# A hybrid encoder layer on one core: the decays between tokens come from running sums read back from DRAM as rows

## The chip, the core and the metric

The kernel runs on one core of a Trainium2 chip. The core has five engines that run their own instruction streams in order and meet through semaphores: TensorE (PE, matrix products into PSUM), VectorE (DVE), ScalarE (ACT), GpSimd (POOL) and SyncE (SP, which here only issues DMAs). The metric is the device time of one execution in microseconds, the median of several runs.

## The reference, cut to what matters

One layer over 256 tokens of width 2048: RMSNorm, a large input projection, three branches (a bidirectional Mamba-2 scan called SSD, a dilated window attention, a Conformer convolution), gates, an output projection and an MLP with squared ReLU. The change is in the SSD branch, which runs once forward and once backward over two chunks of 128 tokens, with 32 heads of 64 channels in 4 groups. For one direction:

```python
def ssd_chunked(xh, dt, a, bm, cm):
    ...
    adt = (dt * a).reshape(bsz, nc, q, ng, nr).transpose(0, 3, 4, 1, 2)
    a_cs = jnp.cumsum(adt, axis=-1)
    seg = a_cs[..., :, None] - a_cs[..., None, :]
    lower = jnp.tril(jnp.ones((q, q), dtype=bool))
    lmat = jnp.exp(jnp.where(lower, seg, -jnp.inf))
    ...
    cb = jnp.einsum("bclgn,bcsgn->bgcls", cc, bc)
    y_diag = jnp.einsum("bgrcls,bcsgrp->bclgrp", cb[:, :, None] * lmat, xdt)
```

`adt` is negative. For tokens l >= s of a chunk the decay is exp(sum of adt over s < i <= l), a 128 x 128 matrix for each head, chunk and direction. The backward direction needs the same with the tokens reversed, so that for one head and chunk the forward decays fill one triangle and the backward decays the other.

## The kernel before

**The stream of weights.** Nearly all of the time goes to matrix products of f32 weights. The weights come in 696 *units* of up to 512 KB (`load`, L1180, a DMA on SP's queue into one of 5 buffers `raw`). `split` (L1196) makes each into a high part on ACT (`hi`, L1211, type f32r, 4 buffers) and a low part, the difference, on DVE (`lo`, L255 through `split_lo`). `mm` (L1227) multiplies three times: high weight by high and low activation, low weight by high activation (L1264 to L1276). The main loop (L1303) does for each unit k: load unit k + 5, split unit k + 3 (`LEAD`), multiply unit k.

**The jobs.** Everything else is written as generators, the *jobs*, which a planner (`Sched`, L79) advances between the units. A job yields what it needs next: "v", "a", "g" or "p" with a number of nanoseconds (credit on DVE, ACT, POOL or PE, which each unit grants anew), "w" (wait so many units), "b" (PSUM banks, of 4), "m" (slabs of SBUF, of 33), "j" (a condition). Jobs of a lower number go first. The order in which instructions are written is fixed when the program is built; each engine then runs its own in that order.

**job_dt** (L368) makes, once, the step sizes `dt` and `adt = dt * a` for all tokens on the partitions and 64 columns (32 heads, two directions). `adt` is then split into `adh` (f32r, ACT, L428) and `adl` (DVE, L431). Four matmuls with triangular masks (L436) give sums over tokens, whose exponentials `sp` (L440) scale what goes from chunk to chunk.

**job_cb** (L773) makes for one group the product of C and B, masked by the two triangles. **job_ssd** (L796) runs for each of the 4 groups and 2 chunks, eight times. It multiplies x by `sp` (`xsx`, L811) on DVE and by the skip factor on POOL (L813), multiplies by the other chunk's part (L819) and adds both into y (L822, L825). Then it goes through its 8 heads in two half-batches of 4 (`hb`, L826). Each half-batch:

- ACT scales the masks LE and GE by `adh`, one column for each head and direction: 8 instructions (L832) into `rh`; DVE does the same with `adl`, 4 heads at a time: 2 instructions (L835) into `rl`.
- PE multiplies four times with the strict masks `gtr` and `ltr` (f32r copies of GT and LT) into one bank (L842). Entry (s, 4 heads x l) of the bank is the sum of adt between s and l: forward above the diagonal, backward below it.
- ACT scales `cb` by the forward `dt` (L846) and takes the exponential of the bank (L849); DVE adds the backward part of `cb` (L854) and multiplies the two (L857).
- PE multiplies by x (L864), DVE adds the result to y (L869).

The jobs of one group run at priority 3; the long convolution on DVE (`job_conv31`, L551) and its LayerNorm run at priority 4 beside them.

Of the kernel before, what the change touches and what calls it, by code (L numbers as in the profile page):

```python
# [20 lines left out]
P = 128  # L21
# [169 lines left out]
def kernel(ctx: ExitStack, tc: tile.TileContext, xT, xn, par, cm, cd, cq, w1, wq, ws, out):  # L191
# [7 lines left out]
    lp = ctx.enter_context(tc.tile_pool(name="lp", bufs=4))  # L199
    pm = ctx.enter_context(tc.tile_pool(name="pm", bufs=2, space=PSUM))  # L200
    pd = ctx.enter_context(tc.tile_pool(name="pd", bufs=BANKS, space=PSUM))
    ctx.enter_context(tc.manual_schedule())
    cnt = [0]

# [31 lines left out]
    V.memset(ones, 1.0)  # L236
    onesd = cp.tile([P, P], F32, name="onesd")
    V.memset(onesd, 1.0 / D)
    ltr = cp.tile([P, P], F32R, name="ltr")
    gtr = cp.tile([P, P], F32R, name="gtr")  # L240
    qgs = cp.tile([P, 1], F32, name="qgs")
    warm = cp.tile([P, 1], F32, name="warm")

# [124 lines left out]
    def job_dt(main):  # L368
# [6 lines left out]
        raw = tmp[:, 5:7, :].rearrange("p a b -> p (a b)")  # L375
        dt = cp.tile([P, 2, 64], F32, name="dt")
        adt = cp.tile([P, 2, 64], F32, name="adt")
        adh = cp.tile([P, 2, 64], F32R, name="adh")
        adl = cp.tile([P, 2, 64], F32, name="adl")
        ea = cp.tile([P, 64], F32, name="ea")  # L380
        sp = cp.tile([P, 4, HEADS], F32, name="sp")
        st.update(dt=dt, adh=adh, adl=adl, sp=sp)
        yield "j", lambda: "r1" in st
        yield "v", 400
        for t in range(2):
# [38 lines left out]
            V.scalar_tensor_tensor(adt[:, t, :], dt[:, t, :], -1.0, ea, op0=ALU.mult, op1=ALU.mult)  # L424
        S.give(2)
        yield "w", 1
        yield "a", 200
        A.activation(adh, adt, AF.Copy)  # L428
        yield "w", 1
        yield "v", 200  # L430
        V.tensor_tensor(adl, adt, adh.bitcast(F32), op=ALU.subtract)  # L431
        yield "b", 1
        ps = bank((4, P))
        yield "p", 900
        for i, m in enumerate((GT, LE, LT, GE)):
            PE.matmul(ps[:, i, :], m, adt.rearrange("p a b -> p (a b)"), start=True, stop=True)  # L436
        yield "w", 1
        yield "a", 1500
        for i, o in enumerate((0, 64, 96, 32)):
            A.activation(sp[:, i, :], ps[:, i, o:o + HEADS], AF.Exp)  # L440
        S.banks += 1
        yield "w", 1
        yield "v", 300
        V.tensor_tensor(sp[:, 0, :], sp[:, 0, :], dt[:, 0, 0:32], op=ALU.mult)
# [351 lines left out]
    def job_ssd(g, c):  # L796

        yield "j", lambda: cbs[g] is not None
        dt, adh, adl, sp = st["dt"], st["adh"], st["adl"], st["sp"]
        yield "m", 4  # L800
        rh = slab([2, 4, P], F32R, name="rh")
        rl = slab([2, 4, P], F32R, name="rl")
        em = slab([2, 4, P], name="em")
        xsx = slab([2, 512], name="xsx")
        cb, x, yy = cbs[g], xs[g], y[g][:, c, :]
# [18 lines left out]
        yield "v", 620  # L824
        V.tensor_tensor(yy, yy, xsx[:, 1, :], op=ALU.add)  # L825
        for hb in range(2):  # L826
            for d in range(2):
                for i in range(4):
                    col = 32 * d + 8 * g + 4 * hb + i
                    msk = LE if d == 0 else GE  # L830
                    yield "a", 290
                    A.activation(rh[:, d, i, :], msk, AF.Copy, scale=adh[:, c, col:col + 1].bitcast(F32))  # L832
                col = 32 * d + 8 * g + 4 * hb
                yield "v", 620
                V.tensor_tensor(rl[:, d], msk[:, None, :].to_broadcast([P, 4, P]),  # L835
                                adl[:, c, col:col + 4][:, :, None].to_broadcast([P, 4, P]), op=ALU.mult)
            yield "w", 1
            yield "b", 1
            ba = bank((4, P))
            yield "p", 900  # L840
            for n, (lt, src) in enumerate(((gtr, rh[:, 0]), (gtr, rl[:, 0]), (ltr, rh[:, 1]), (ltr, rl[:, 1]))):
                PE.matmul(ba, lt, src, start=(n == 0), stop=(n == 3))  # L842
            for i in range(4):
                yield "a", 290
                col = 8 * g + 4 * hb + i
                A.activation(em[:, 1, i, :], cb[:, c, :], AF.Copy, scale=dt[:, c, col:col + 1])  # L846
            yield "w", 1
            yield "a", 500
            A.activation(em[:, 0], ba, AF.Exp)  # L849
            S.banks += 1  # L850
            for i in range(4):
                yield "v", 270
                col = 32 + 8 * g + 4 * hb + i
                V.scalar_tensor_tensor(em[:, 1, i, :], cb[:, 2 + c, :], dt[:, c, col:col + 1], em[:, 1, i, :],  # L854
                                       op0=ALU.mult, op1=ALU.add)
            yield "v", 620
            V.tensor_tensor(em[:, 0], em[:, 0], em[:, 1], op=ALU.mult)  # L857
            yield "w", 1
            yield "b", 1
            bd = bank((4, P))  # L860
            yield "p", 880
            for i in range(4):
                pr = 256 * hb + 128 * (i // 2)
                PE.matmul(bd[:, i, :], em[:, 0, i, :], x[:, c, pr:pr + P], start=True, stop=True)  # L864
            yield "w", 1
            yield "v", 400
            bv = bd.rearrange("p (q r) e -> p q (r e)", q=2).rearrange("p q (s e) -> p q s e", s=4)[:, :, 0::3, :]
            yv = yy[:, 256 * hb:256 * hb + 256].rearrange("p (q s e) -> p q s e", q=2, s=2)
            V.tensor_tensor(yv, yv, bv, op=ALU.add)  # L869
            S.banks += 1  # L870
# [432 lines left out]
    for k in range(NU):  # L1303
# [9 lines left out]
            nc.scalar.dma_start(dist, cd)  # L1313
        elif k == 8:
            V.tensor_scalar(qgs, par_("qg"), P ** -0.5, None, op0=ALU.mult)
            A.activation(ltr, LT, AF.Copy)
            A.activation(gtr, GT, AF.Copy)
        split(k + LEAD)
        mm(k)
        bi, u = units[k]  # L1320
# [80 lines left out]
```

## Time and profile before

| | |
|---|---|
| median of 3 runs | 1981.73 us |
| lowest and highest | 1981.35 and 1984.19 us |
| the profiled execution | 1983.86 us |
| its span, first to last instruction | 1982.1 us |
| TensorE clock granted, mean | 0.999 |
| moved by DMA | 364.51 MB, 184 GB/s |

The profile is of one execution. Its page gives, for each engine, the busy time and its share of the span; then the span in 40 equal slices, each with a digit for the tenths of the slice in which the engine was busy; then the chain of work that ended last, followed back from the last instruction. A row of a group reads: line, engine, operation, output <- inputs, shapes, count | busy us, mean ns of one | idle time of the engine just before. Instructions of one engine overlap a little, so that busy time can be less than count times mean. A row of the waits reads: who waited <- for whom: us in total, times, longest us. A row of a timeline reads: start us, duration us, engine, line, operation. Lines are those of the kernel printed above.

### The profile page before, as it was taken

Reading aid. Unit: us, or ns where it says so; the run is one execution under the profiler, and the core shown is the slowest. Engines: PE = TensorE matmul, PEld = TensorE weight load, DVE = VectorE, ACT = ScalarE, POOL = GpSimd, SP = SyncE. Lnnn points to the kernel's source line nnn. Section 1 sums busy time; section 2 is a strip of 40 time slices with the busy share of each in tenths; the row PEclk is TensorE's granted clock in tenths of the full one; section 3 lists DMA queues with packets and bytes.
Section 4 is the critical chain, followed back from the end, with each engine's and each line's share of the span. In section 5 each row is a group of like instructions: output and inputs, shape, how many; then the busy total and the mean of one; then the engine's idle time right before and its main releaser. Section 6 shows DMA issues by size and latency. Waiting matters only on the chain.

```text
span 1982.1 us, 29949 instructions
## 1 busy us (share of the span) xinstructions
PE 1966.0 (99%) x11798; PEld 1766.0 (89%) x11798; DVE 1309.0 (66%) x1847; ACT 1036.0 (52%) x1446; POOL 47.5 (2%) x42
## 2 busy tenths in 40 slices
PE   8999999999999999999999999999999999999999
PEld 7999999999998888888888888999988998998887
DVE  5778887887887889896654555555555554455443
ACT  6654576777757655545654444544443443344332
POOL 0000010000000000003000000000000000000000
PEclk9999999999999999999999999999999999999999
DMA  8555554554554555555555556555555555555554
GB/s 284 184 175 183 165 185 145 167 172 144 184 170 161 176 181 178 183 191 187 190 191 183 189 189 207 194 186 192 188 190 189 189 191 191 188 186 191 190 181 149
DMA packets 105342, 364.51 MB, mean 184 GB/s; under 512 B 11760, under 2 KB 12272, under 8 KB 105200
## 3 DMA queue, kind: packets, MB, share of 16 engines
q1 hardware_dynamic: 103904, 360.23, 55.4%
q10 hardware_dynamic: 1296, 2.36, 0.3%
q8 instruction: 92, 1.51, 0.3%
q14 instruction: 50, 0.41, 0.1%
HBM read 360.45 MB, written 2.10 MB: 183 GB/s over the span
## 4 chain that ended last, share of the span: by engine, by line
PE 95%; DVE 0%; issue 0%
PE main L1273 19%; PE main L1274 19%; PE main L1276 19%; PE main L1266 11%; PE main L1264 11%; PE main L1268 11%; PE b L842 1%; PE b L864 1%; PE b L968 1%; PE b L1273 0%; PE b L1274 0%; PE b L1276 0%; PE b L819 0%; PE b L501 0%; PE b L757 0%; PE b L742 0%
## 5 line engine op out<-in xcount | busy, mean ns | idle before, releaser
L255 DVE TENSOR_TENSOR lo<-raw,hi 128x1024 fp32r<-128x1024 f32 (+2 forms) x697 | 831.5, 1194 | 643.5 <-ACT hi L1211 638.7
L1211 ACT ACTIVATE hi<-raw 128x1024 fp32r<-128x1024 f32 (+2 forms) x695 | 716.2, 1032 | 868.7 <-PE main L1274 487.8
L1273 PE MATMUL main<-hi,hh 128*128 128x512 f32 (+1 forms) x800 | 306.1, 383 | 0.0
L1274 PE MATMUL main<-hi,hl 128*128 128x512 f32 (+1 forms) x800 | 299.0, 374 | 0.0
L1266 PE MATMUL main<-x2l,hi 128*128 128x256 f32 x1024 | 246.4, 281 | 0.0
L1264 PE MATMUL main<-x2h,hi 128*128 128x256 f32 x1024 | 246.3, 279 | 0.0
L1266 PE MATMUL main<-hl,hi 128*128 128x256 f32 x896 | 216.3, 281 | 3.2 <-DVE hl L255 3.2
L1264 PE MATMUL main<-hh,hi 128*128 128x256 f32 x896 | 217.7, 282 | 0.0
L565 DVE SCALAR_TENSOR_TENSOR co<-cin,cpar,co 128x256 f32<-128x256 f32 x480 | 211.1, 491 | 0.0
L1276 PE MATMUL main<-lo,hh 128*128 128x512 f32 (+1 forms) x800 | 200.5, 372 | 0.0
L1264 PEld LDWEIGHTS main<-x2h,hi 128*128 128x128 f32 x1024 | 192.7, 188 | 0.2
L1266 PEld LDWEIGHTS main<-x2l,hi 128*128 128x128 f32 x1024 | 192.6, 188 | 0.2
L1273 PE MATMUL main<-hi,ah 128*128 128x512 f32 x480 | 188.9, 394 | 0.0
L1274 PE MATMUL main<-hi,al 128*128 128x512 f32 x480 | 188.6, 393 | 0.0
L1273 PEld LDWEIGHTS main<-hi,hh 128*128 128x128 f32 x800 | 152.5, 191 | 23.4 <-ACT hi L1211 1.2
L1274 PEld LDWEIGHTS main<-hi,hl 128*128 128x128 f32 x800 | 152.2, 190 | 22.9 <-issue 1.9
L1266 PEld LDWEIGHTS main<-hl,hi 128*128 128x128 f32 x896 | 168.8, 188 | 4.2 <-DVE hl L255 3.6
L1264 PEld LDWEIGHTS main<-hh,hi 128*128 128x128 f32 x896 | 169.2, 189 | 0.6
L1276 PEld LDWEIGHTS main<-lo,hh 128*128 128x128 f32 x800 | 148.0, 190 | 22.1
L1268 PE MATMUL main<-x2h,lo 128*128 128x256 f32 x1024 | 138.3, 277 | 0.0
L1276 PE MATMUL main<-lo,ah 128*128 128x512 f32 x480 | 130.1, 393 | 0.0
L1268 PEld LDWEIGHTS main<-x2h,lo 128*128 128x128 f32 x1024 | 127.6, 188 | 0.0
(244 smaller groups left out, 2304.5 us busy)
## 6 DMA issues: line engine op xcount, KB each, us to landing
raw<-ws_dram SPq DMA_DIRECT2D x600, 512.0 KB, 3.3
raw<-wq_dram SPq DMA_DIRECT2D x88, 384.0 KB, 3.1
raw<-w_dram SPq DMA_DIRECT2D x7, 448.0 KB, 7.0
xr<-xn_dram SPq DMA_DIRECT2D x4, 512.0 KB, 9.2
x<-xn_dram SPq DMA_DIRECT2D x4, 512.0 KB, 4.3
xt<-xT_dram SPq DMA_DIRECT2D x7, 256.0 KB, 7.0
out_dram<-x SPq DMA_DIRECT2D x4, 256.0 KB, 3.7
out_dram<-x ACTq DMA_DIRECT2D x4, 256.0 KB, 5.6
```

What stands on the lines that cost most here:

```text
L255: V.tensor_tensor(lo, raw, hi.bitcast(F32), op=ALU.subtract)
L565: V.scalar_tensor_tensor(dst[:, e, :], x[:, e, k:k + T], par_("dw", (2 * i + e) * 31 + k), dst[:, e, :], op0=ALU.mult, op1=ALU.add)
L842: PE.matmul(ba, lt, src, start=(n == 0), stop=(n == 3))
L864: PE.matmul(bd[:, i, :], em[:, 0, i, :], x[:, c, pr:pr + P], start=True, stop=True)
L968: PE.transpose(b[:, e, t * P:t * P + P], src[:, t, k * P:k * P + P], ID)
L1211: A.activation(h, r, AF.Copy)
L1264: PE.matmul(o, wh[:, e, cs], ah, start=(first and e == 0 and c % 2 == 0), stop=False, skip_group_check=True)
L1266: PE.matmul(o, wh[:, e, cs], al, start=False, stop=False, skip_group_check=True)
L1268: PE.matmul(o, wl[:, e, cs], ah, start=False, stop=(last and e == 1), skip_group_check=True)
L1273: PE.matmul(o, ah[:, xs_], wh[:, e, :], start=(first and e == 0), stop=False)
L1274: PE.matmul(o, al[:, xs_], wh[:, e, :], start=False, stop=False)
L1276: PE.matmul(o, ah[:, xs_], wl[:, e, :], start=False, stop=(last and e == 1))
```

## The change

The running sums themselves are made once, in job_dt, by two more matmuls with the inclusive masks LE and GE, in the other orientation: column q of `adt` on partition q, tokens along the row (`pr`, then `rows` in SBUF). A DMA on ACT's queue writes them to a DRAM tile `sums` of 2 x 128 x 128 f32 (direction, chunk and column, token). The negated sums with tokens on the partitions are kept as `nsum`, from two of the four matmuls that were there.

Each job_ssd starts with four DMAs on POOL's queue: for each half-batch and direction the rows of 4 heads, 2 KB, go to all 128 partitions (256 KB in SBUF) in `fr`, now one slab for each half-batch. In a half-batch ACT adds the negated sum of the partition's own token to the backward rows (4 instructions), DVE adds it to the forward rows and takes the minimum of the two (4 instructions): of the two differences one is negative in one triangle, the other in the other. The exponential reads this from SBUF. The scaled masks (L832, L835), the four matmuls (L842) and their bank go, and so do `adh`, `adl`, `ltr` and `gtr`.

```diff
--- before.py
+++ after.py
@@ -199,6 +199,7 @@
     lp = ctx.enter_context(tc.tile_pool(name="lp", bufs=4))
     pm = ctx.enter_context(tc.tile_pool(name="pm", bufs=2, space=PSUM))
     pd = ctx.enter_context(tc.tile_pool(name="pd", bufs=BANKS, space=PSUM))
+    dp = ctx.enter_context(tc.tile_pool(name="dp", bufs=1, space=bass.MemoryType.DRAM))
     ctx.enter_context(tc.manual_schedule())
     cnt = [0]
 
@@ -236,8 +237,6 @@
     V.memset(ones, 1.0)
     onesd = cp.tile([P, P], F32, name="onesd")
     V.memset(onesd, 1.0 / D)
-    ltr = cp.tile([P, P], F32R, name="ltr")
-    gtr = cp.tile([P, P], F32R, name="gtr")
     qgs = cp.tile([P, 1], F32, name="qgs")
     warm = cp.tile([P, 1], F32, name="warm")
 
@@ -375,11 +374,11 @@
         raw = tmp[:, 5:7, :].rearrange("p a b -> p (a b)")
         dt = cp.tile([P, 2, 64], F32, name="dt")
         adt = cp.tile([P, 2, 64], F32, name="adt")
-        adh = cp.tile([P, 2, 64], F32R, name="adh")
-        adl = cp.tile([P, 2, 64], F32, name="adl")
+        nsum = cp.tile([P, 2, 2, HEADS], F32, name="nsum")
+        sums = dp.tile([2, P, P], F32, name="sums")
         ea = cp.tile([P, 64], F32, name="ea")
         sp = cp.tile([P, 4, HEADS], F32, name="sp")
-        st.update(dt=dt, adh=adh, adl=adl, sp=sp)
+        st.update(dt=dt, nsum=nsum, sums=sums, sp=sp)
         yield "j", lambda: "r1" in st
         yield "v", 400
         for t in range(2):
@@ -424,21 +423,27 @@
             V.scalar_tensor_tensor(adt[:, t, :], dt[:, t, :], -1.0, ea, op0=ALU.mult, op1=ALU.mult)
         S.give(2)
         yield "w", 1
-        yield "a", 200
-        A.activation(adh, adt, AF.Copy)
-        yield "w", 1
-        yield "v", 200
-        V.tensor_tensor(adl, adt, adh.bitcast(F32), op=ALU.subtract)
-        yield "b", 1
+        yield "b", 2
         ps = bank((4, P))
-        yield "p", 900
+        pr = bank((2, T))
+        yield "p", 1340
         for i, m in enumerate((GT, LE, LT, GE)):
             PE.matmul(ps[:, i, :], m, adt.rearrange("p a b -> p (a b)"), start=True, stop=True)
-        yield "w", 1
-        yield "a", 1500
+        for d, m in enumerate((LE, GE)):
+            PE.matmul(pr[:, d, 0:P], adt.rearrange("p a b -> p (a b)"), m, start=True, stop=True)
+        yield "m", 1
+        rows = slab([2, P], name="rows")
+        yield "w", 1
+        yield "a", 2600
+        A.activation(rows, pr[:, :, 0:P], AF.Copy)
+        nc.scalar.dma_start(sums.rearrange("d q j -> q d j"), rows)
+        for d in range(2):
+            A.activation(nsum[:, :, d, :], ps[:, 1 + 2 * d, :].rearrange("p (t x) -> p t x", t=2)[:, :, 32 * d:32 * d + 32],
+                         AF.Copy, scale=-1.0)
         for i, o in enumerate((0, 64, 96, 32)):
             A.activation(sp[:, i, :], ps[:, i, o:o + HEADS], AF.Exp)
-        S.banks += 1
+        S.banks += 2
+        S.give()
         yield "w", 1
         yield "v", 300
         V.tensor_tensor(sp[:, 0, :], sp[:, 0, :], dt[:, 0, 0:32], op=ALU.mult)
@@ -796,10 +801,13 @@
     def job_ssd(g, c):
 
         yield "j", lambda: cbs[g] is not None
-        dt, adh, adl, sp = st["dt"], st["adh"], st["adl"], st["sp"]
+        dt, nsum, sp = st["dt"], st["nsum"], st["sp"]
         yield "m", 4
-        rh = slab([2, 4, P], F32R, name="rh")
-        rl = slab([2, 4, P], F32R, name="rl")
+        fr = [slab([2, 4, P], name="fr") for _ in range(2)]
+        for hb in range(2):
+            for d in range(2):
+                q = 64 * c + 32 * d + 8 * g + 4 * hb
+                nc.gpsimd.dma_start(fr[hb][:, d], st["sums"][d:d + 1, q:q + 4, :].to_broadcast([P, 4, P]))
         em = slab([2, 4, P], name="em")
         xsx = slab([2, 512], name="xsx")
         cb, x, yy = cbs[g], xs[g], y[g][:, c, :]
@@ -824,30 +832,22 @@
         yield "v", 620
         V.tensor_tensor(yy, yy, xsx[:, 1, :], op=ALU.add)
         for hb in range(2):
-            for d in range(2):
-                for i in range(4):
-                    col = 32 * d + 8 * g + 4 * hb + i
-                    msk = LE if d == 0 else GE
-                    yield "a", 290
-                    A.activation(rh[:, d, i, :], msk, AF.Copy, scale=adh[:, c, col:col + 1].bitcast(F32))
-                col = 32 * d + 8 * g + 4 * hb
-                yield "v", 620
-                V.tensor_tensor(rl[:, d], msk[:, None, :].to_broadcast([P, 4, P]),
-                                adl[:, c, col:col + 4][:, :, None].to_broadcast([P, 4, P]), op=ALU.mult)
+            f = fr[hb]
+            for i in range(4):
+                yield "a", 290
+                A.activation(f[:, 1, i, :], f[:, 1, i, :], AF.Identity, bias=nsum[:, c, 1, 8 * g + 4 * hb + i:8 * g + 4 * hb + i + 1])
             yield "w", 1
-            yield "b", 1
-            ba = bank((4, P))
-            yield "p", 900
-            for n, (lt, src) in enumerate(((gtr, rh[:, 0]), (gtr, rl[:, 0]), (ltr, rh[:, 1]), (ltr, rl[:, 1]))):
-                PE.matmul(ba, lt, src, start=(n == 0), stop=(n == 3))
+            for i in range(4):
+                yield "v", 270
+                V.scalar_tensor_tensor(em[:, 0, i, :], f[:, 0, i, :], nsum[:, c, 0, 8 * g + 4 * hb + i:8 * g + 4 * hb + i + 1],
+                                       f[:, 1, i, :], op0=ALU.add, op1=ALU.min)
             for i in range(4):
                 yield "a", 290
                 col = 8 * g + 4 * hb + i
                 A.activation(em[:, 1, i, :], cb[:, c, :], AF.Copy, scale=dt[:, c, col:col + 1])
             yield "w", 1
             yield "a", 500
-            A.activation(em[:, 0], ba, AF.Exp)
-            S.banks += 1
+            A.activation(em[:, 0], em[:, 0], AF.Exp)
             for i in range(4):
                 yield "v", 270
                 col = 32 + 8 * g + 4 * hb + i
@@ -1313,8 +1313,6 @@
             nc.scalar.dma_start(dist, cd)
         elif k == 8:
             V.tensor_scalar(qgs, par_("qg"), P ** -0.5, None, op0=ALU.mult)
-            A.activation(ltr, LT, AF.Copy)
-            A.activation(gtr, GT, AF.Copy)
         split(k + LEAD)
         mm(k)
         bi, u = units[k]
```

## The prediction

> **What bounds the kernel.** I read, in this order, the page's busy times and slices, the chain of waits by line, and then the stages in which the changed lines run.
>
> ```profile
> PE 1966.0 (99%) x11798; PEld 1766.0 (89%) x11798; DVE 1309.0 (66%) x1847; ACT 1036.0 (52%) x1446; POOL 47.5 (2%) x42
> PE   8999999999999999999999999999999999999999
> PE 95%; DVE 0%; issue 0%
> by line: PE main L1273 19.0%; PE main L1274 19.0%; PE main L1276 18.9%; PE main L1266 11.3%; PE main L1264 11.1%; PE main L1268 11.1%; PE b L842 0.7%; PE b L864 0.7%; PE b L968 0.5%; PE b L1273 0.4%; PE b L1274 0.4%; PE b L1276 0.4%; PE b L
> core 0: us, PE busy (x) PEld busy (x) DVE busy (x) ACT busy (x) POOL busy (x), PEclk, DMA share, GB/s
> 300.00:400.00 100.00, 100.00 (x704) 98.14 (x703) 78.11 (x152) 68.86 (x142) 3.66 (x2) 1.00 0.50 153
> ...
> 700.00:760.00 60.00, 60.00 (x272) 49.20 (x271) 52.08 (x87) 31.94 (x45) 0.00 (x0) 1.00 0.52 176
> sum 460.00, PE 460.00 PEld 425.11 DVE 371.90 ACT 304.52 POOL 14.74; mean PE 92.00 PEld 85.02 DVE 74.38 ACT 60.91 POOL 2.95
> ```
>
> TensorE (PE) is busy in 99% of the span, in all 40 slices but the first at nine tenths or more, and 95% of the chain that ended last is PE work. The stage table (first and last of five stages, and their sum) is for the stretch in which nearly all of the SSD jobs fall: there PE is busy 460.0 of 460.0 us, while VectorE (DVE) has 371.9 and ScalarE (ACT) 304.5, and the DMA engines are half used. So whatever leaves PE there shortens the span, and whatever joins DVE, ACT or the queues costs nothing until PE has to wait for it. The line that the change deletes, L842, stands in the chain with 0.7%, which is 12.9 to 14.9 us (0.65 to 0.75% of 1982.1).
>
> How far are DVE and ACT ahead of PE? The waits say:
>
> ```profile
> DVE lo L255 <- ACT hi L1211: 638.7, 551, 8.4
> ACT hi L1211 <- PE main L1274: 487.8, 319, 2.6
> POOL xsx L813 <- ACT xs L688: 464.5, 5, 252.1
> ACT hi L1211 <- PE main L1266: 308.1, 191, 3.0
> 724.03 1.06 ACT L1211 ACTIVATE hi<-raw 128x1024 fp32r<-128x1024 f32 x1 [1.72 <-PE main L1274]
> 726.82 1.06 ACT L1211 ACTIVATE hi<-raw 128x1024 fp32r<-128x1024 f32 x1 [0.56 <-PE main L1274]
> L255 DVE TENSOR_TENSOR lo<-raw,hi 128x1024 fp32r<-128x1024 f32 (+2 forms) x697 | 831.5, 1194 | 643.5 <-ACT hi L1211 638.7 <-PE main L1268 2.1 <-ACT hi L1208 1.6
> ```
>
> 510 of the 695 weight splits (L1211) found ACT waiting for PE to give back one of the four "hi" buffers. So the splits run as far ahead as the buffers allow. The two timeline rows are 2.79 us apart, one weight unit. A split that starts when PE finishes with its buffer has the rest of that unit and the three units in between: at least 3 x 2.79 = 8.4 us until PE needs it, less 1.06 us on ACT and 1.19 us on DVE (L255), leaves 6.2 us. An ACT or DVE stall shorter than that, once, does not reach PE. POOL is busy 47.5 us in all; its queue comes further down.
>
> **What the change removes from PE.** In each of 8 SSD jobs (4 groups by 2 chunks) and each of its 2 half-batches (hb), four matmuls of 512 columns (L842) made the exponents: 8 x 2 x 4 = 64. What each costs on the path is not its duration, since matmuls overlap, but the step from start to start:
>
> ```profile
> 298.64 0.39 PE L842 MATMUL b<-rh,gtr 128*128 128x512 f32 x1
> 298.87 0.39 PE L842 MATMUL b<-rl,gtr 128*128 128x512 f32 x1
> ...
> 299.32 0.40 PE L842 MATMUL b<-rl,ltr 128*128 128x512 f32 x1
> 299.56 0.28 PE L1264 MATMUL main<-hh,hi 128*128 128x256 f32 x1
> L842 PE MATMUL b<-rh,gtr 128*128 128x512 f32 x16 | 6.4, 398 | 0.0
> 106.70 1.05 PE L436 MATMUL b<-adt,cmask 128*128 128x128 f32 x8
> 107.52 0.36 PE L1264 MATMUL main<-hh,hi 128*128 128x256 f32 x1
> ```
>
> Four of them push the next weight matmul from 298.64 to 299.56, 0.92 us; 16 such sets make 14.7 us. That agrees with the chain's 12.9 to 14.9. Their mean duration of 398 ns would give 64 x 0.398 = 25.5 us, but PE accepts the next after 230 ns, so I take 14.7.
>
> **What it adds to PE.** Two matmuls of 128 columns in job_dt, the running sums laid out as rows. Four of that form (eight passes, L436) take from 106.70 to 107.52, 0.82 us, so two take 0.41 us. Net on PE: 14.7 - 0.4 = 14.3 us less.
>
> **What moves on DVE and ACT.**
>
> ```profile
> L832 ACT ACTIVATE rh<-cmask,adh 128x128 fp32r<-128x128 f32 x128 | 42.0, 398 | 0.0
> L835 DVE TENSOR_TENSOR rl<-cmask,adl 128x512 fp32r<-128x512 f32 x32 | 21.8, 684 | 0.0
> L854 DVE SCALAR_TENSOR_TENSOR em<-cb,dt,em 128x128 f32<-128x128 f32 x64 | 18.5, 345 | 0.0
> 0.74 0.41 ACTq L224 DMA_DIRECT2D cpar<-par_dram  x1
> ```
>
> DVE loses the 32 products of L835 (21.8 us busy) and gains 64 scalar_tensor_tensor of 128x128, for which the 64 of L854 in the same shape are the row: 18.5 us. ACT loses 128 scaled masks (42.0 us busy) and gains 64 biased copies of the same shape: 21.0 us. The Exp of L849 stays, reading SBUF and not PSUM, 16 times. So DVE loses 3 us and ACT 21 us, neither on the path: they make splits no later. Once, at about 107 us, ACT gets one 128x256 copy out of PSUM, two small ones and a DMA issue: by 398 ns for each 128x128 piece and 0.41 us for an issue (the ACT-queue row) some 4 x 0.40 + 0.41 = 2.0 us, a third of the 6.2 us of cover. DVE loses adl there, and the two conversions of LT and GT go. The extra bank and slab in job_dt can delay only what waits for "dt_done", and that is first used by a job_cb some 150 us later. All of this I cost at nothing; what hides it is the lead of the splits, and if that were gone for this one moment, it would cost 2 us.
>
> **The new wait: rows that come back from DRAM.** Each SSD job issues four DMAs of 256 KB on POOL's queue, 32 in all, 8.4 MB over some 480 us, 17 GB/s on top of the stage's 153 to 176. The trace has no DMA issued by POOL and none that reads one row into all partitions, so I bound the time to landing by plain loads of the same size:
>
> ```profile
> dist<-cd_dram ACTq DMA_DIRECT2D x1, 256.0 KB, 11.0
> perm<-cq_dram ACTq DMA_DIRECT2D x1, 256.0 KB, 3.2
> 673.11 0.69 DVE L811 TENSOR_TENSOR xsx<-xs,sp 128x512 f32<-128x512 f32 x1
> 684.38 1.27 ACT L832 ACTIVATE rh<-cmask,adh 128x128 fp32r<-128x128 f32 x4
> 610.26 1.05 POOL L813 TENSOR_TENSOR xsx<-xs,cpar 128x512 f32<-128x512 f32 x1 [8.96 <-PE b L742]
> 252.52 1.91 POOL L813 TENSOR_TENSOR xsx<-xs,cpar 128x512 f32<-128x512 f32 x1 [252.08 <-ACT xs L688]
> 0.00:20.00 20.00, 17.44 (x69) 15.20 (x70) 12.21 (x23) 13.71 (x24) 0.20 (x4) 1.00 0.87 315
> ```
>
> 256 KB landed in 3.2 us alone on ACT's queue (perm) and in 11.0 us (dist) behind the two loads that the code issues on it just before. The DMA engines moved 315 GB/s in the first 20 us (last row), so the stage's 176 has room for 17 more. In the last job 11.3 us pass between its first DVE work (L811 at 673.11) and the first line that will need a row (L832's place, 684.38); the code issues the DMAs ahead of L811. POOL is usually further ahead still: the first xsx product ran at 252.52, and POOL had waited 252 us with nothing else to do. The four DMAs stand in front of that product in its queue and need neither xs nor anything else but a free slab and the written sums (107 us, long past). A slab still being read is possible: the product at 610.26 had waited 9 us for a matmul (L742) that was reading its slab. Behind the four DMAs on POOL stand xsx (needed by L825) and the LayerNorm additions (L263), whose sum the LayerNorm takes up long after the SSD stage.
>
> So hb 0, which needs two DMAs, has 11.3 us before ACT stalls at all and 11.3 + 6.2 = 17.5 us before PE does. By the low row two in sequence take 6.4 us, by the high row 22.0. I take a value near the low row: POOL's queue is empty, which is the case of the 3.2, while the 11.0 stood in line. Hence no stall, and the term is 0. The high row goes into a rival.
>
> A page of the Trainium skill speaks against this. "SBUF — State Buffer", section "A bandwidth-pool intuition that's wrong (but worth ruling out)", lists DRAM as reached through 32 ports of about 22.5 GB/s each. If the 2 KB that all 128 partitions ask for lie behind one port, a 256 KB transfer would take an estimated 11.7 us by that figure, and the sum would come out as in rival A below, a loss. No row of the trace shows such a read, so it can't be weighed here; the sum goes by the rows above.
>
> **Sum.** The profiled execution took 1983.86 us (span 1982.1 and 1.8 around it): 1983.9 - 14.3 = 1969.6. It lies 2.1 us above the median of the runs shown, so for the median I forecast 1981.7 - 14.3 = 1967.4 us, 0.7% less.
>
> **Rivals.** *A, slower: the rows land late.* If every transfer takes the 11.0 us of the high row, one after the other, hb 0 is complete after 22.0 us, 4.5 us after PE's cover has ended. In 8 jobs that is 36 us of PE waiting, against 14.3 won: 1981.7 - 14.3 + 36 = 2003 us. It turns into a loss when the stall passes 14.3 / 8 = 1.8 us a job, that is when two transfers take over 17.5 + 1.8 = 19.3 us, 9.7 each or 27 GB/s. For it: 128 partitions ask for the same 2 KB of DRAM, no row shows such a read, and the ACT instruction that waits has weight splits queued behind it. Against it: POOL's head start, and that hb 1 has more time than hb 0. The port figure of the Trainium skill's page "SBUF — State Buffer", named above, would bring this rival about. Chance 0.13.
>
> *B, part of the gain is lost.* Different costs in the planner shift all later jobs by a slot or so, and PE meets a few new waits of the kind that it has today:
>
> ```profile
> PE b L296 <- DVE dg L291: 4.1, 1, 4.1
> PE main L1266 <- DVE hl L255: 3.2, 2, 2.2
> ```
>
> At 2 to 4 us each, two or three of them give back 4 to 10 us: about 1974. For it: DVE is busy for 52.1 of 60 us at the end of the stage, so a clump of work there delays splits. Against it: the job's DVE and ACT work gets less. Chance 0.11.
>
> *C, no change.* The PE time is freed, but PE then waits the same time at L864 for an exponential that now comes off a longer ACT-DVE-ACT-DVE path: about 1980. Against it: L849 was already waiting on PE, and two of the waiting slots between the steps stay. Chance 0.04.
>
> **How the numbers follow.** The forecast has 0.72. A difference of under 0.2% (4 us; the runs shown spread over 2.8) can't be told from no change. Faster: forecast and B, 0.83, less a little for the tails: 0.82. Same: 0.05. Slower: A, 0.13. The range runs from 1962 (the 14.3, and 5 of the 16 us in which PE is idle today, 1982.1 - 1966.0, recovered by the shifted order) to 1977 (B at its worst, 10 us lost). That holds forecast and B, about 0.8; A lies outside.
>
> **What would show it.** Right: no L842 group; PE still 99% busy; the chain without the line; L813 and the new adds without long waits on DMA; DMA from POOL landing in 3 to 6 us; span near 1968. Step by step: 64 matmuls fewer and 2 more, DVE busy about 3 us less, ACT 21 us less. Wrong: ACT or DVE rows that name the DMA "fr" as releaser with over 17 us behind the issue; PE idle in slices 5 to 14; "hi" splits waiting on DMA and not on PE; DVE at 95% or more in the stage.

## The result and the profile after

The changed kernel took 1969.14 us (median of 4 runs, 1969.02 to 1971.88) and the kernel before 1981.68 us beside it (1981.35 to 1984.19): a ratio of 0.9937, with a 95% interval of 0.992 to 0.9955. That is 12.5 us less. The profiled execution took 1971.88 us (span 1970.1), 12.0 us less than the profiled execution of before.

The page of the changed kernel, from its busy times and its chain of waits:

```profile
span 1970.1 us, 29877 instructions
PE 1956.2 (99%) x11738; PEld 1760.6 (89%) x11738; DVE 1305.7 (66%) x1878; ACT 1012.3 (51%) x1379; POOL 66.8 (3%) x74
PE 95%; DVE 0%; issue 0%
```

TensorE is still busy in 99% of the span and still makes 95% of the chain. There are 60 fewer matmuls in the records, where 64 went and two, in four passes, came. ScalarE is busy 23.7 us less (1036.0 to 1012.3), VectorE 3.3 us less (1309.0 to 1305.7). The stage table, with the columns of before:

```profile
core 0: us, PE busy (x) PEld busy (x) DVE busy (x) ACT busy (x) POOL busy (x), PEclk, DMA share, GB/s
300.00:400.00 100.00, 100.00 (x707) 98.60 (x706) 80.22 (x159) 64.33 (x131) 7.55 (x10) 1.00 0.58 180
...
sum 460.00, PE 460.00 PEld 425.17 DVE 380.27 ACT 289.76 POOL 28.46; mean PE 92.00 PEld 85.03 DVE 76.05 ACT 57.95 POOL 5.69
```

In the SSD stage PE is busy 460.0 of 460.0 us, as before. So no new wait reached it there, and what left PE shortened the stage. The rows of the new tile `fr` and the waits of the changed kernel (who waited <- for whom: us, times, longest) say how near a wait came:

```profile
L838 ACT ACTIVATE fr<-fr,nsum x64: 383/388/441, 287.5 to 679.3; 128x128 f32<-128x128 f32 x64
L842 DVE SCALAR_TENSOR_TENSOR em<-fr,nsum x64: 340/346/353, 292.0 to 683.6; 128x128 f32<-128x128 f32 x64
L810 POOL DMA_DIRECT2D fr<-sums x32: 538/538/703, 107.4 to 601.5; - x32
DMA to landing us min/median/max: 4.0/5.9/11.5
```

```profile
ACT hi L1211 <- PE main L1274: 484.0, 309, 2.6
ACT hi L1211 <- PE main L1266: 305.9, 183, 3.5
POOL fr L810 <- PE main L1266: 107.0, 1, 107.0
POOL fr L810 <- DVE em L854: 62.4, 1, 62.4
POOL fr L810 <- ACT hi L1211: 44.3, 1, 44.3
```

A transfer landed 4.0 to 11.5 us after its issue. No ACT or DVE row names it as the one waited for. It is the other way round: POOL stood ready and waited 107, 62 and 44 us for a free slab or for the written sums. The splits still wait for PE to give back their buffer (492 times), so they still run as far ahead as they can. How early the rows were there is told by the timelines of POOL and of ACT:

```profile
107.42 4.42 POOL L810 DMA_DIRECT2D fr<-sums  x8 [106.98 <-PE main L1266]
...
586.93 2.17 POOL L810 DMA_DIRECT2D fr<-sums  x4
```

```profile
610.66 1.27 ACT L838 ACTIVATE fr<-fr,nsum 128x128 f32<-128x128 f32 x4
```

The first eight transfers were issued from 107.42 on and first used at 287.5 (L838 above). The narrowest case is the four issued from 586.93 on, 23.7 us before ACT took the first of them at 610.66.

**Where the 12.0 us came from.** Four lines that both kernels have cut the span: the transpositions of x for the SSD groups (L685, now L690), those of y behind the SSD jobs (L968), and in the MLP the squared ReLU (L1053) and the additions to the output (L1073). First of before, then of after; "a to b" are the first and last starts:

```profile
L685 PE MATMUL b<-cmask,xq x32: 270/272/273, 251.2 to 597.0; 128*128 128x128 f32 x32
L968 PE MATMUL b<-cmask,y x32: 271/272/273, 754.3 to 830.0; 128*128 128x128 f32 x32
L1053 DVE SCALAR_TENSOR_TENSOR u<-main,rbc x32: 681/682/685, 1289.4 to 1802.3; 128x512 f32<-128x512 f32 x32
L1073 DVE TENSOR_TENSOR x<-x,main x24: 678/680/683, 1467.9 to 1890.9; 128x512 f32<-128x512 f32 x24
```

```profile
L690 PE MATMUL b<-cmask,xq x32: 270/272/274, 251.6 to 592.0; 128*128 128x128 f32 x32
L968 PE MATMUL b<-cmask,y x32: 270/272/273, 740.1 to 815.7; 128*128 128x128 f32 x32
L1053 DVE SCALAR_TENSOR_TENSOR u<-main,rbc x32: 681/684/687, 1274.2 to 1791.0; 128x512 f32<-128x512 f32 x32
L1073 DVE TENSOR_TENSOR x<-x,main x24: 678/681/684, 1454.3 to 1879.6; 128x512 f32<-128x512 f32 x24
```

By first starts: before the SSD stage the changed kernel is 0.4 us late (251.6 against 251.2). Behind the stage it is 14.2 us early (740.1 against 754.3), at the start of the MLP (L1053) 15.2 us, and at the last start of L1073 only 11.3 us. So the stage gave 14.6 us, and the MLP, whose code is the same in both kernels, took 605.4 us (1274.2 to 1879.6) where it had taken 601.5 (1289.4 to 1890.9). It gave 3.9 us back. Another 1.0 us was won between L968 and the MLP, and 0.7 us behind the last L1073: 0.4 - 14.6 - 1.0 + 3.9 - 0.7 = -12.0 us. The loss in the MLP is what the experiments had to explain, beside the theory itself.

### The profile page after: what moved, and what is told of

Same layout as the page of the kernel before. It is cut to its first block, busy times and chain, and to the rows that moved or that the text cites. A ratio compares the mean times of both kernels' runs of the same rounds, so it can differ in the third digit from the quotient of the medians.

```text
span 1970.1 us, 29877 instructions
## 1 busy us (share of the span) xinstructions
PE 1956.2 (99%) x11738; PEld 1760.6 (89%) x11738; DVE 1305.7 (66%) x1878; ACT 1012.3 (51%) x1379; POOL 66.8 (3%) x74
## 4 chain that ended last, share of the span: by engine, by line
PE 95%; DVE 0%; issue 0%
PE main L1274 19%; PE main L1273 19%; PE main L1276 19%; PE main L1266 11%; PE main L1268 11%; PE main L1264 11%; PE b L864 1%; PE b L968 1%; PE b L1273 0%; PE b L1276 0%; PE b L1274 0%; PE b L827 0%; PE b L506 0%; PE b L762 0%; PE b L690 0%; PE b L747 0%
## 5 line engine op out<-in xcount | busy, mean ns | idle before, releaser
L1273 PE MATMUL main<-hi,hh 128*128 128x512 f32 (+1 forms) x800 | 305.1, 381 | 0.0
L1264 PE MATMUL main<-x2h,hi 128*128 128x256 f32 x1024 | 247.5, 280 | 0.0
L1266 PE MATMUL main<-x2l,hi 128*128 128x256 f32 x1024 | 247.2, 281 | 0.0
L1266 PE MATMUL main<-hl,hi 128*128 128x256 f32 x896 | 217.1, 282 | 3.1 <-DVE hl L254 3.1
L1264 PE MATMUL main<-hh,hi 128*128 128x256 f32 x896 | 218.9, 283 | 0.0
L1264 PEld LDWEIGHTS main<-x2h,hi 128*128 128x128 f32 x1024 | 193.0, 188 | 0.2
L1266 PEld LDWEIGHTS main<-x2l,hi 128*128 128x128 f32 x1024 | 192.6, 188 | 0.2
L1273 PE MATMUL main<-hi,ah 128*128 128x512 f32 x480 | 188.7, 393 | 0.0
L1273 PEld LDWEIGHTS main<-hi,hh 128*128 128x128 f32 x800 | 152.5, 191 | 23.1 <-ACT hi L1211 1.0
L1266 PEld LDWEIGHTS main<-hl,hi 128*128 128x128 f32 x896 | 169.5, 189 | 3.6 <-DVE hl L254 3.5
L1264 PEld LDWEIGHTS main<-hh,hi 128*128 128x128 f32 x896 | 169.8, 189 | 0.0
L1268 PE MATMUL main<-x2h,lo 128*128 128x256 f32 x1024 | 140.5, 279 | 0.0
L1268 PEld LDWEIGHTS main<-x2h,lo 128*128 128x128 f32 x1024 | 128.9, 188 | 0.0
```

Of the source, the lines that this page charges most:

```text
L1264: PE.matmul(o, wh[:, e, cs], ah, start=(first and e == 0 and c % 2 == 0), stop=False, skip_group_check=True)
L1266: PE.matmul(o, wh[:, e, cs], al, start=False, stop=False, skip_group_check=True)
L1268: PE.matmul(o, wl[:, e, cs], ah, start=False, stop=(last and e == 1), skip_group_check=True)
L1273: PE.matmul(o, ah[:, xs_], wh[:, e, :], start=(first and e == 0), stop=False)
```

## The experiments

The theory was the one predicted: what is won is TensorE time, and the rows cost nothing because they are requested long before they are used. The rivals were that the rows' transfers cost something that the profile hides, and, for the MLP, several ideas of what makes the same code slower.

**again**: the changed kernel unaltered, for its spread and for the MLP.

> The changed kernel, unaltered, once more, with a second profile. The shift of the weight matmuls against the kernel before was -14.2 us at the end of the SSD stage, as summed, but only -12.0 at the end of the span: in the MLP the steps between the 256-column weight matmuls are 117.5 ns on average against 116.4 before. If these steps are a property of the kernel (of where its tiles lie), the second profile shows 117.5 again; if they wander from one execution to the next, it shows another value, 116 to 118. Time about 1969.1 us either way.

It took 1970.35 us (1969.04 to 1971.3); ratio 0.9936, interval 0.9921 to 0.9951. The stretch from the first L1053 to the last L1073 took 605.5 us (1273.6 to 1879.1) again. The 3.9 us are therefore a property of this program and not of one execution.

**pad**: an unused tile of 1.5 KB a partition, so that the slabs begin at the address in SBUF that they had before the change.

```diff
     qgs = cp.tile([P, 1], F32, name="qgs")
+    padt = cp.tile([P, 384], F32, name="padt")
...
         elif k == 8:
+            V.memset(padt, 0.0)
```

> The changed kernel with an unused tile of 1.5 KB per partition, so that the slabs begin at the address that they had before the change. If the slabs' base address makes the MLP's steps longer, they go back from 117.5 to 116.4 ns and the time falls by some 3 us to about 1966. If not, the time stays at 1969.1 within 1 us.

1971.5 us (1969.29 to 1972.07), ratio 0.994, interval 0.9926 to 0.9955, and 605.4 us for the stretch of the MLP. The time lies within what executions of one kernel differ by, and the moved start of the slabs is not the cause.

**pe_back**: the work of PE alone comes back. In each half-batch four f32r matmuls of 512 columns, on an old activation tile, go into a bank that nothing reads.

```diff
             yield "w", 1
+            yield "b", 1
+            ba = bank()
+            yield "p", 900
+            hh = st["h"][0][0].rearrange("p a b -> p (a b)")
+            for n in range(4):
+                PE.matmul(ba, hh[:, n * P:n * P + P], hh[:, 0:512], start=(n == 0), stop=(n == 3))
+            S.banks += 1
             for i in range(4):
                 yield "v", 270
```

> The changed kernel with four matmuls of 512 columns put back in each half-batch where the removed ones stood, on operands that are there anyway, into a bank that nobody reads: 64 in all. If the gain is TensorE's time and nothing else, 64 x 0.23 = 14.7 us come back: 1969.1 + 14.7 = 1983.8 us. The rival, that ACT's 64 instructions fewer or the freed bank made the kernel faster, expects it to stay below 1975.

1982.59 us (1980.68 to 1983.98, 10 runs), ratio 0.9998, interval 0.9989 to 1.0007: the whole gain is gone. The group of the added matmuls, and the rows that cut the span (behind the edit, this kernel's lines lie 7 further on):

```profile
L845 PE MATMUL b<-hh 128*128 128x512 f32 x64 | 17.5, 395 | 0.0
```

```profile
L690 PE MATMUL b<-cmask,xq x32: 270/272/273, 248.6 to 577.8; 128*128 128x128 f32 x32
L1060 DVE SCALAR_TENSOR_TENSOR u<-main,rbc x32: 678/682/684, 1286.6 to 1799.2; 128x512 f32<-128x512 f32 x32
L1080 DVE TENSOR_TENSOR x<-x,main x24: 678/680/681, 1464.5 to 1887.8; 128x512 f32<-128x512 f32 x24
```

From L690 to the MLP it takes 1038.0 us (1286.6 - 248.6), 15.4 us more than the changed kernel's 1022.6 and nearly the 1038.2 of before. The stretch of the SSD jobs alone can be cut out by the weight matmuls, since every kernel here has the same 11,232 in the same order: from the start of the 1,687th (at 250.2 us before) to that of the 4,488th (760.1) it takes 509.9 us before, 495.3 in the changed kernel and 510.1 here. The added matmuls cost 14.8 us there. The rows' DMAs, the new copies and the new additions are all still there. The edit brings back the use of a PSUM bank and a place in the planner too, but in none of the three kernels is PE idle in that stretch, so what the stage gained is TensorE time. And this kernel's MLP takes 601.2 us (1887.8 - 1286.6), as that of before. That is most of why the medians move by 12.2 us from `again` and not by 15.4.

**no_dma**: the 32 row transfers go, and ACT and DVE read tiles of constants in their place, so the decays are left out of this kernel's result.

```diff
-        for hb in range(2):
-            for d in range(2):
-                q = 64 * c + 32 * d + 8 * g + 4 * hb
-                nc.gpsimd.dma_start(fr[hb][:, d], st["sums"][d:d + 1, q:q + 4, :].to_broadcast([P, 4, P]))
...
-                A.activation(f[:, 1, i, :], f[:, 1, i, :], AF.Identity, bias=nsum[...])
+                A.activation(f[:, 1, i, :], cmask[:, 1 + i, :], AF.Identity, bias=par_("dtb", 8 * g + 4 * hb + i))
...
-                V.scalar_tensor_tensor(em[:, 0, i, :], f[:, 0, i, :], nsum[...],
+                V.scalar_tensor_tensor(em[:, 0, i, :], cmask[:, 1 + i, :], par_("dtb", 8 * g + 4 * hb + i),
```

> The changed kernel without the 32 DMAs that bring the rows back (the sums are still written to DRAM); ACT and DVE read a constant tile in the place of the rows, in the same shapes and number, so the decays are left out. If the transfers are covered, as the theory has it, the time stays at 1969.1 within 1 us. The rival, that the 1.8 us between the forecast (1967.4) and the result went to the transfers, expects 1967 to 1967.5.

1969.98 us (1968.6 to 1970.06), ratio 0.9933, interval 0.9916 to 0.9949. Without the transfers the kernel is 0.4 us faster than `again`, less than either one's spread, and the stretch of the SSD jobs takes 495.2 us with no row transfers and 495.3 with them. They cost nothing that can be measured.

**jit**: the same transfers with the head start taken away. DVE writes one element in each of the two parts (forward and backward) of the half-batch's slab when the half-batch begins, and the two DMAs of that half-batch, which overwrite it, are issued only then.

```diff
         for hb in range(2):
             f = fr[hb]
+            V.memset(f[:, :, 0, 0:1], 0.0)
+            for d in range(2):
+                q = 64 * c + 32 * d + 8 * g + 4 * hb
+                nc.gpsimd.dma_start(f[:, d], st["sums"][d:d + 1, q:q + 4, :].to_broadcast([P, 4, P]))
             for i in range(4):
```

(and the four DMAs at the head of the job go)

> The changed kernel with POOL's head start taken away: the two DMAs of a half-batch can't be issued before DVE has written one element per head slab in program order, at the half-batch's first instruction, so ACT meets them right behind their issue (32 issues as before; 16 tiny DVE writes more). ACT then waits about a landing (median 5.9 us in the changed kernel) in each of 16 half-batches, with weight splits queued behind it. The theory puts 6.2 us of cover between such a stall and PE: PE loses under 1 us a time, 1969 to 1980 us in all. The rival, that each wait for rows reaches PE in full (no cover), expects 16 x 5.9 = 94 us more, 2060 us.

2001.45 us (2000.27 to 2005.31), ratio 1.0091, interval 1.0076 to 1.0106: some 31 us more than the changed kernel, and a loss against before. Neither expectation held. The waits of ACT for rows, then all waits of PE from 280 to 800 us:

```profile
ACT fr L838 <- DMA fr<-sums: 74.7, 13, 10.5
```

```profile
PE b L864 <- DVE em L857: 15.4, 6, 6.4
PE b L747 <- ACT sc L740: 3.8, 1, 3.8
PE main L1273 <- ACT sg L933: 3.1, 1, 3.1
PE main L1264 <- ACT hi L1211: 1.3, 2, 0.7
```

ACT now stops for rows 13 times, up to 10.5 us. The damage was expected at the weight splits, which stand behind ACT's wait. They hardly hurt: PE waits for `hi` 1.3 us in this stretch. It waits 15.4 us at L864 for L857, the product of a half-batch, and once each at a matmul of the attention (L747) and at a weight matmul (L1273), for ACT instructions (L740, L933) that stand behind an L838 that waits. Three timelines, of ACT, DVE and PE, show the longest wait:

```profile
434.49 1.28 ACT L838 ACTIVATE fr<-fr,nsum 128x128 f32<-128x128 f32 x4 [9.71 <-DMA fr<-sums]
...
446.77 0.98 ACT L838 ACTIVATE fr<-fr,nsum 128x128 f32<-128x128 f32 x3 [5.99 <-DMA fr<-sums]
...
448.60 0.61 ACT L850 ACTIVATE em<-em 128x512 f32<-128x512 f32 x1
```

```profile
437.90 1.13 DVE L842 SCALAR_TENSOR_TENSOR em<-fr,nsum 128x128 f32<-128x128 f32 x4
...
451.11 0.69 DVE L857 TENSOR_TENSOR em<-em 128x512 f32<-128x512 f32 x1
```

```profile
451.95 2.05 PE L864 MATMUL b<-xs,em 128*128 128x128 f32 x8 [6.42 <-DVE em L857]
```

The planner placed L864 in PE's order by the time that the chain before it normally takes (ACT, DVE, ACT, DVE). The two jobs of a group run beside each other. The half-batch of this L864 has its rows at 434.49 and its differences (L842) at 437.90. Its exponential (L850), however, stands in ACT's order behind the L838 of the other job, which waits 5.99 us for rows of its own. So L850 comes at 448.60, L857 at 451.11, and PE, which had come to L864 6.42 us earlier, stops there with every weight matmul behind it. At other places, as for the 2.8 us up to 668.4, it is the half-batch's own rows that are late. The stage table of this kernel, in stretches of 40 us:

```profile
320.00:360.00 40.00, 36.20 (x265) 35.89 (x264) 28.11 (x61) 21.76 (x39) 1.06 (x2) 0.91 0.42 137
...
400.00:440.00 40.00, 38.25 (x296) 37.62 (x295) 26.59 (x53) 24.42 (x47) 2.23 (x5) 1.00 0.57 187
440.00:480.00 40.00, 33.58 (x243) 33.30 (x242) 30.12 (x62) 21.56 (x38) 0.96 (x2) 0.91 0.47 153
...
640.00:680.00 40.00, 35.29 (x219) 31.81 (x218) 32.32 (x62) 21.61 (x32) 2.29 (x3) 0.91 0.50 172
...
720.00:760.00 40.00, 38.30 (x163) 31.14 (x164) 36.07 (x60) 20.43 (x26) 1.59 (x1) 0.96 0.56 197
...
sum 520.00, PE 496.41 PEld 457.11 DVE 398.51 ACT 306.70 POOL 33.49; mean PE 38.19 PEld 35.16 DVE 30.65 ACT 23.59 POOL 2.58
```

PE is idle 23.6 of the 520 us (520.00 - 496.41), which is the sum of the four rows of its waits above. In the stretches with 3.8 to 6.4 us idle the granted clock (third column from the end) falls to 0.91; with 1.8 us in two stops (the second row) it stays at 1.00. The 0.96 of the fifth row follows a stop of 3.1 us that began in the stretch before, at 718.6. In shorter stretches the clock stands at 0.50 for 6.8 us three times (from 329.8, 449.3 and 667.8 us on) and for 3.4 us once (from 722.4 on): (3 x 6.8 + 3.4) x 0.50 = 11.9 us of lost full-speed time. Together that is 35.5 us. From the 1,687th to the 4,488th weight matmul this kernel takes 530.9 us, 35.6 more than the changed kernel's 495.3. The Trainium skill, "TensorE: Matmul & The Clock Gate", section "Part 1: The HAM clock gate (the "warmup" mystery)", says that the array falls to half its clock after an idle window of about 3.4 us and returns after as long a busy one. The trace agrees with the half clock and with its length, one or two times 3.4 us, but the stops of 2.8 us (at 665.6) and 3.1 us (at 718.6) that brought it on are shorter than such a window.

**sp_queue** and **act_queue**: the same DMAs at the same places, issued by SP and by ACT in place of POOL.

```diff
-                nc.gpsimd.dma_start(fr[hb][:, d], ...)
+                nc.sync.dma_start(fr[hb][:, d], ...)     (sp_queue)
+                nc.scalar.dma_start(fr[hb][:, d], ...)   (act_queue)
```

> The changed kernel with the 32 row DMAs on SP's queue, between the weight loads. SP comes to them in step with the weight buffers, so it waits for a slab only as long as the slab's last reader lags behind SP, some units at most, and the weight loads behind have about 10 us in hand (five buffers): the theory expects 1969 to 1973 us. The rival, that the weight stream stands still while a row DMA waits for its slab as POOL's queue did (62, 44 and 9 us in the changed kernel's trace), expects over 2000 us.

> The changed kernel with the 32 row DMAs on ACT's queue. Each issue takes ACT 0.4 to 0.5 us, 13 to 16 us in all, which its idle time hides; a wait for a slab now holds up the weight splits behind it, with 6.2 us of cover. The theory expects 1969 to 1975 us: slower than POOL's queue only where a slab's last reader is a matmul that is still to come. The rival, that issuing on an engine's own queue costs nothing at all, expects 1969 with ACT waits unchanged.

sp_queue took 1971.96 us (1971.12 to 1973.14), ratio 0.9939, interval 0.9924 to 0.9954; act_queue 1971.02 us (1970.27 to 1972.52), ratio 0.9935, interval 0.992 to 0.995. The rows of the tile, first on SP's queue, then on ACT's:

```profile
L810 SPq DMA_DIRECT2D fr<-sums x32: 320/430/2044, 259.1 to 635.4; - x32
DMA to landing us min/median/max: 4.0/6.0/8.0
```

```profile
L810 ACTq DMA_DIRECT2D fr<-sums x32: 326/454/1866, 263.6 to 643.0; - x32
DMA to landing us min/median/max: 3.2/6.6/8.4
```

The first request comes some 150 us later than on POOL, because SP and ACT have other work in their order ahead of it. The time from issue to landing is nearly the same. Both times lie in the ranges that the theory gave, and the rival of sp_queue, over 2000 us, is refuted. The rival of act_queue, that ACT's waits stay as they are, is refuted too, and the medians hide a cost there. The issues themselves held ACT up once, and the splits behind them:

```profile
267.07 6.46 ACTq L810 DMA_DIRECT2D fr<-sums  x3
273.58 1.58 ACT L1211 ACTIVATE hi<-raw 128x768 fp32r<-128x768 f32 x2 [7.47 <-DMA fr<-sums]
```

A stop of 7.47 us is longer than the 6.2 us of the splits' lead, and PE then waited 1.5 us for `hi`. What the issues waited for isn't shown. From the 1,687th to the 4,488th weight matmul act_queue takes 498.5 us, 3.2 more than the changed kernel; sp_queue takes 496.1. In act_queue's median this doesn't show because its MLP happens to be 2.5 us shorter (602.9 against 605.4). So POOL's free queue was worth some 3 us against ACT's.

**swap**, **swap_act**, **spin**: three ideas on the MLP's 3.9 us. Two exchange slabs that the MLP stage takes, so that its operands lie elsewhere; one shifts the whole stream by one more matmul at the start.

```diff
-        h = slab([4, T], F32R, name="x2h")
         l = slab([4, T], F32R, name="x2l")
+        h = slab([4, T], F32R, name="x2h")      (swap, job_x2)
...
+        l = slab([4, T], F32R, name="al")
         u = slab([4, T], name="u")
         h = slab([4, T], F32R, name="ah")
-        l = slab([4, T], F32R, name="al")       (swap_act, job_up)
...
-    for _ in range(7):
+    for _ in range(8):                          (spin)
```

> The changed kernel with one exchange in job_x2: the slab for the low part x2l is taken before that for the high part x2h, so that the two swap their places in SBUF; nothing else in any engine's stream changes. If the length of the MLP's matmul steps (117.5 ns here, 116.4 before) hangs on which slabs the activations lie in, it changes, to somewhere between 113 and 119 ns, that is by up to some 13 us in the time either way. If it doesn't change, the cause lies elsewhere.

> The changed kernel with the order of the three slabs in job_up changed (low part, then u, then high part), so that in the MLP ACT and DVE write, and the down blocks read, other slabs than before; no instruction is added, moved or dropped. The exchange of x2h and x2l left the MLP's steps at 117.5 ns to the last digit. If the place of what is written beside the 256-column matmuls sets their step, it changes now, by 0.3 ns or more, which is about 1 us in the time; if it stays at 117.5, slabs are not the cause.

> The changed kernel with eight warm-up matmuls and not seven at the start, so that every later TensorE instruction stands one matmul further along in its stream and nothing else changes. If the MLP's steps hang on where the instructions lie in the stream, they move away from 117.5 ns by 0.3 ns or more; if not, they stay at 117.5, and the time stays within the 2 to 3 us by which executions of one kernel differ.

swap took 1970.21 us (1968.84 to 1972.22), ratio 0.9933, interval 0.9917 to 0.995; swap_act, in one run, 1969.04 and spin, in one run, 1970.67. The MLP's stretch took 605.5 us in swap (1271.1 to 1876.6), 605.5 in swap_act (1271.3 to 1876.8) and 605.4 in spin (1273.0 to 1878.4). None of the three changes it. No kernel tried is measurably faster than the changed one.

## Why the prediction was right, point by point

**The PE term** was exact. 64 steps of 0.23 us made 14.7; the stage gave 14.6, and pe_back, which brings as many matmuls back, costs 14.8 in the same stretch. Counting steps from start to start, and not the 25.5 us of summed durations, is what made the term right.

**The two new matmuls** were put at 0.41 us. They run in two passes each:

```profile
102.08 0.61 PE L433 MATMUL b<-cmask,adt 128*128 128x128 f32 x4
102.44 0.37 PE L1264 MATMUL main<-hh,hi 128*128 128x256 f32 x1
```

The four passes push the next weight matmul from 102.08 to 102.44, 0.36 us. That the changed kernel is just 0.4 us late at L690 is no proof of it: other executions with the same early work come to L690 between 248.6 (swap) and 251.8 us (pad).

**DVE and ACT** were to lose 3 and 21 us of work off the path: 3.3 and 23.7 measured, and no wait of PE for either in the stage.

**The rows** were taken near the low bound of 3.2 to 11.0 us. The median of 5.9 lies between, the longest, 11.5, a little above. The conclusion held with much room, but not for the reasons given. Two transfers in sequence at the median would take 11.8 us, more than the 11.3 that the prediction gave them before ACT stalls. The time ahead was not 11.3 us but 23.7 at the least, since POOL runs further ahead than the job. And the 6.2 us of the splits' lead, which the prediction added on top, hold for the splits (act_queue shows it) but do not protect the small matmuls whose own operands pass through ACT: in jit, waits of up to 10.5 us on ACT came out as waits of up to 6.4 us on PE, at L864. Neither error decided anything here, because the rows were there in time.

**Rival A** (rows late) did not come about by itself; jit, which takes the head start away, ends at 2001.45 us, beside the 2003 that A was given. That is luck, for the way there was another: 23.6 us idle, 15.4 of them at L864 and only 1.3 behind late splits, and 11.9 us of lowered clock, not 4.5 us a job. The transfers' own speed refutes the figure that would have brought A about. Eight of them, issued from 107.42 to 111.84 us, had all landed by 123.3 us at the latest (111.84 + 11.5): 2.1 MB in 15.9 us, over 130 GB/s, beside the weights. By the page "SBUF — State Buffer" of the Trainium skill, section "A bandwidth-pool intuition that's wrong (but worth ruling out)", DRAM has 32 ports of about 22.5 GB/s each. The prediction's estimate from that figure, with one row behind one port, was 11.7 us for each transfer. The median of 5.9 us speaks against one port serving such a read.

**Rival B** (part of the gain lost to new waits) was wrong in its mechanism: PE has no new waits in the stage. A loss at the low end of its size (3.9 us, where it had 4 to 10) came in another place. The step of the prediction that failed is the unsaid one, that code which the change doesn't touch takes as long as before: the MLP took 3.9 us more, which with the gains of 1.0 and 0.7 us on either side of it left 12.0 us of the 14.3 forecast. **Rival C** (PE waits at L864 instead) is refuted by the stage table, 460.0 of 460.0.

What makes the MLP slower stays open. Of the 3.9 us, 3.3 lie in the weight matmuls of 256 columns (L1264, L1266, L1268): their mean step from start to start is 117.5 ns in the changed kernel and 116.4 before, at a granted clock of 1.00 and with PE always busy in both. Six programs (the changed kernel itself, again, pad, swap, swap_act, spin) need 605.4 or 605.5 us for the stretch, whatever their addresses and their start. The others need 601.2 (pe_back), 601.5 (before), 602.9 (act_queue), 603.7 (jit), 603.8 (no_dma) and 606.7 (sp_queue). It is not PE's order of work: act_queue, sp_queue, jit and no_dma have the changed kernel's 11,738 PE instructions in the same order, and act_queue and sp_queue those of DVE, ACT and POOL too, save for the issues of the row transfers. What these four change is how or whether the rows are fetched, over 500 us ahead of the MLP. The stretch is the same in each execution of the six that was profiled, and no busy row or wait accounts for it. Which detail does it was not found.

## What to carry to other kernels

When one engine is full, cost an edit by the steps of that engine alone, and measure them from the start of one instruction to the start of the next. A transfer through DRAM is free if its request stands in a queue that runs far ahead; check the time from request to use. If it can be late, look for the victim at every instruction of the full engine whose operands pass through the engine that waits, not only at the main work behind the wait. Expect some 0.2% either way from code that you did not touch, and compare the same instructions stage by stage, since such a shift can hide a cost in the median.

## What was unexpected of the hardware

The MLP's same 605 us came back to 0.1 us in six programs that fetch the rows in the same way, and moved between 602.9 and 606.7 us when only the queue that issues the row transfers was changed, over 500 us earlier.

The executions of one kernel differ by 2 to 3 us, and part of that is settled in the first 100 us. Two stretches of the changed kernel, then the same two of swap, which does the same work (the granted clock is the third column from the end):

```profile
40.00:60.00 20.00, 20.00 (x107) 19.88 (x106) 12.89 (x34) 12.11 (x35) 0.00 (x0) 0.88 0.51 155
...
80.00:100.00 20.00, 17.83 (x136) 17.52 (x135) 14.76 (x31) 6.24 (x6) 0.00 (x0) 0.91 0.49 159
```

```profile
40.00:60.00 20.00, 20.00 (x115) 19.76 (x115) 14.14 (x38) 11.90 (x35) 0.00 (x0) 0.96 0.52 172
...
80.00:100.00 20.00, 17.83 (x149) 17.52 (x148) 15.03 (x30) 7.91 (x9) 0.00 (x0) 1.00 0.47 168
```

In the changed kernel's profiled execution PE had a lower clock there than in that of swap: 0.08 x 20 + 0.09 x 20 = 3.4 us of full-speed time less. At L690 it is 3.0 us behind swap (251.6 against 248.6) and stays so to the end (spans of 1970.1 and 1967.1).

POOL needed 0.54 us to issue one of the row transfers (538/538/703 ns min, median and longest of 32), although DVE was busy for 80 of 100 us beside some of them (from 300 to 400 us).
